# Second block: VectorE in program order, and what waits for ScalarE emitted later

## The chip, the cores and the metric

The kernel runs on one core of a Trainium2 chip. The metric is the device time of one launch in microseconds; a figure for a kernel is the median of its runs. TensorE (PE) multiplies matrices and transposes, VectorE (DVE) and ScalarE (ACT) work element by element, GpSimd (POOL) does some of that too, and SyncE (SP) issues the loads and stores. A matmul writes to one of eight PSUM banks, from which VectorE and ScalarE read.

## The reference, cut to what matters

Two transformer-like blocks run one after the other on x of shape (1, 512, 1024), in float32. The first has an RMS norm, a mixer (a chunked mLSTM beside stick-breaking attention) and an MLP with a squared ReLU. The change lies in the second, which is attention in three branches over 16 heads and 4 groups of keys and values:

```python
def second_block(x, ...):
    u = rms_norm_2(h, pre_norm_gain[layer])
    y = nsa_mixer(u, ...)
    return h + rms_norm_2(y, post_norm_gain[layer])

def nsa_mixer(h, w_in, w_out, k_pos, k_w1, k_w2, v_pos, v_w1, v_w2, table):
    q, kv, g, z = split_cols(h @ w_in, [NSA_WIDTH, 6 * NSA_KV_WIDTH, 3 * H, 3 * NSA_WIDTH])
    k_c, v_c, k_s, v_s, k_w, v_w = [a.reshape(B, S, G, dh) for a in jnp.split(kv, 6, axis=-1)]
    gates = jax.nn.sigmoid(g).reshape(B, S, 3, H, 1)
    zs = jax.nn.silu(z).reshape(B, S, 3, H, dh)
    kc = compress_kv(k_c, k_pos, k_w1, k_w2)      # blocks of 32 positions, silu(flat @ w1) @ w2
    vc = compress_kv(v_c, v_pos, v_w1, v_w2)
    o_cmp, p_cmp = nsa_compressed(q, kc, vc, table)
    sel = select_blocks(p_cmp, S)
    o_slc = nsa_selected(q, k_s, v_s, sel, table)
    o_win = nsa_window(q, k_w, v_w, table)
    o = jnp.stack([o_cmp, o_slc, o_win], axis=2)
    y = jnp.sum(gates * o * zs, axis=2).reshape(B, S, NSA_WIDTH)
    return y @ w_out
```

At 512 positions the selected branch takes all blocks and the window covers all earlier positions, so both are plain causal attention with a bias by distance, each with its own keys and values.

## The kernel before

**Matmuls in three parts.** To keep float32 accuracy each operand is split in a high half (a rounded copy) and a low half (what is left), and a product is three matmuls: high by high, high by low, low by high. Weights come in tiles of 128 by 1024: SyncE starts the load (tile wr), ScalarE makes the high half (wh, L171), VectorE the low half (wl, L173), from the 143rd tile on GpSimd in VectorE's place.

**Order.** A scheduler lays out the instructions of each engine by its own estimate of when they can run, which need not be the order in which the code emits them. The second block, nsa(), stands under `tc.manual_schedule` for TensorE and GpSimd: these two run in the order of the code there. VectorE, ScalarE and SyncE are laid out by the scheduler.

**The start of nsa().** The code first opens its pools, which lie in memory that the MLP's pools have left, and emits the memset of gz (L838) and two operations that fill gsel (tt, recorded at the helper's line 292). Much later come enter(0) and enter(1), each for half of the positions. enter adds two sums of squares (q), takes a mean (rsm, L286), has GpSimd raise it to the power -1/2 (rsr), scales the input in place (xbig, L284), has TensorE transpose it (L814) and splits the result into ah (ScalarE, L299) and al (VectorE, L289). The first three projections run half by half (half_step, L828). keys_evac, queries_evac and values move projections out of PSUM and split them (w2t at L852 is one such copy). attention() then clears the upper parts of two bias tiles (bt, L1290) and starts its loop.

**The loop of attention().** 8 pairs of heads, 2 branches, 2 heads and 4 blocks of 128 queries make 128 ticks. In a tick, u.scores multiplies queries by keys into one of two banks (L1213, L1214), VectorE adds the bias and takes the row minimum (nm, L1216), and ScalarE takes the exponential (P, L1219). Then come half of the tick's filler work, the flip of the block from two ticks earlier, the other half, and the mix of a half that was flipped at least MLAG ticks ago. A flip transposes P into one of two banks (L1233), ScalarE copies the high half into ptall (L1236), VectorE subtracts for the low half (ptall, L292). A mix multiplies with the values (L1249); after its second half ScalarE copies one part of the result (t1, L1255) and VectorE adds the other, the join. attended(p) then lets GpSimd multiply the pair's output with its gate.

**The filler** is the rest of the block, cut into steps of about 650 ns of TensorE. project(p, br) makes the gate z of a pair and a branch: a projection (three matmuls per weight tile, L332 to L334), a tanh on ScalarE (z, L991), and one VectorE operation (stt, recorded at L289) that multiplies it with the projection. compress makes 16 additions on VectorE (F_) for each of keys and values, four to a tile, while project(0, 1) and project(0, 2) run. cmp_scores, cmp_shift, cmp_exp, cmp_gate and cmp_flip are the compressed branch. Once a pair has all its row sums (dn), gate_rows takes the reciprocal (gs, L1118), multiplies with the gates and writes gz; gate_flip transposes gz (L1131) and gate_scale multiplies z by it. Such jobs wait in a list until a condition holds, counted in filler ticks; `started` is set after the second of the two compress stretches.

**The end.** The output projection's squares (ScalarE), row means m and products with the gain (yg, VectorE), GpSimd's power, and the sum with the residual.

Of the kernel before, what the change touches and what calls it, by code (L numbers as in the profile page):

```python
# [251 lines left out]
def tile_blocks(ctx, tc, x, xt, wts, prm, cst, table, post_g, w2k, w2v, out):  # L252
# [528 lines left out]
    def nsa(x2, ssq2):  # L781
# [4 lines left out]
        with ExitStack() as pts:  # L786
# [195 lines left out]
            def project(p, br):  # L982
                if (p, br) in zt:
                    return
                while live[0] == ZB:
                    yield None
                live[0] += 1
                z = pt.tile([128, T], F32, name="z", tag="z", bufs=ZB)

                def evac(ps):  # L990
                    s.activation(z, ps, AF.Tanh, scale=0.5)  # L991
                    stt(z, z, 1.0, ps, OP.add, OP.mult)
                yield from gen_t(pj, acts, evac)
                zt[p, br] = z
# [64 lines left out]
            def cmp_exp(gq):  # L1059
                P = pct["p", gq]  # L1060
                s.activation(P, P, AF.Exp, scale=-1.0)
                v.reduce_sum(den[:, :, 4 * gq:4 * gq + 4], P.rearrange("p (t r) c -> p t r c", t=4), AX.X)

            def cmp_gate(gq):
                P = pct["p", gq]
                r = small([128, 4, 4], "rgc")
                h4 = slice(4 * gq, 4 * gq + 4)
                v.reciprocal(r, den[:, :, h4])
                tt(r, r, gn[:, :, h4])
                tt(P, P, r.rearrange("p t r -> p (t r)")[:, :, None].to_broadcast([128, 16, 32]))  # L1070
# [129 lines left out]

            class Unit:
# [21 lines left out]
                def flip(self, tb):  # L1223
# [13 lines left out]
                    tt(PTl[:, 0:tb + 1, 128 * i:128 * i + 128], src, hi.bitcast(F32), OP.subtract)  # L1237

                def mix(self, half):
# [12 lines left out]
                    if half == 1:  # L1252
                        a = slice(0, 64) if self.h % 2 == 0 else slice(64, 128)
                        b = slice(64, 128) if self.h % 2 == 0 else slice(0, 64)
                        s.copy(self.t1[a, :], o[a, :])  # L1255
                        tt(self.t1[a, :], self.t1[a, :], o[b, :], OP.add)

            def attention(fill):
# [13 lines left out]
                def mixes(limit=MLAG):  # L1272
                    if len(pend_mix) > 0 and (tick[0] >= pend_mix[0][2] + limit):
                        u, half, _ = pend_mix.pop(0)
                        u.mix(half)
                        if u.h % 2 == 1 and u.br == 1 and half == 1:
                            attended(u.h // 2, u.ots)
# [22 lines left out]
                for p in range(8):  # L1300
# [8 lines left out]
                    for br in range(2):  # L1309
                        t1 = pt.tile([128, T], F32, name="t1", tag="ot", bufs=4)  # L1310
                        ots.append(t1)
                        for e in range(2):
                            u = Unit(2 * p + e, br, bt, t1, dn)
                            u.ots = ots
                            for tb in range(4):
# [3 lines left out]
                                u.scores(tb)  # L1319
                                fill.run(ns / 2)  # L1320
                                new = flips(LAG)
                                fill.run(ns / 2)
                                mixes()
# [4 lines left out]
                    fill.soon(lambda p=p, dn=dn: p - 1 in gated and started[0], lambda p=p, dn=dn: gate_rows(p, dn))  # L1328
                while pend_flip or pend_mix:
                    tick[0] += 1  # L1330
                    new = flips(0)
                    fill.run(ns)
                    mixes()
                    pend_mix += new

# [23 lines left out]
        with tc.tile_pool(name="pf", bufs=1) as pf:  # L1359
# [8 lines left out]
            for c in range(2):  # L1368
                ps = proj_n(pj, ys, 1 + 2 * c)
                for tb in range(4):  # L1370
# [4 lines left out]
                    step = v.tensor_scalar(m, ssq[:, c, tb:tb + 1], 1.0 / D, EPS if c == 0 else means[tb],  # L1375
                                           OP.mult, OP.add)
                    if c == 0:
                        means.append(m)
                        tt(yg[:, tb, cs], ps[tb], gb_[:, cs])
                    else:  # L1380
                        with tc.issue_after(step.ins):
                            tt(yg[:, tb, cs], ps[tb], gb_[:, cs])
# [9 lines left out]
    with tc.manual_schedule(engines={mybir.EngineType.PE, mybir.EngineType.Pool}):  # L1392
        nsa(xb, sums2)
# [55 lines left out]
```

## Time and profile before

| what | value |
|---|---|
| median of 3 runs | 1370.91 us (1369.25, 1370.91, 1371.4) |
| the profiled execution | 1371.08 us |
| its span in the trace | 1369.4 us |
| mean granted TensorE clock, share of full speed | 0.993 |
| TensorE busy | 1324.5 us, 97% |
| VectorE busy | 720.9 us, 53% |
| ScalarE busy | 655.6 us, 48% |
| GpSimd busy | 273.8 us, 20% |

The span runs from the first to the last instruction that the profiler recorded; the 1.7 us by which the execution is longer lie around it. The first block ends, and the second begins, at about 870 us. Busy shares are means over all stages. What the time depends on is read from the windows and the order of time, where an instruction's idle time before it stands in brackets with what released it.

### The profile page before, as it was taken

To read this page: it belongs to the slowest core of one execution; us is meant where nothing else is said; L and a number is where in the kernel's file an instruction comes from. 1 tells how busy PE (TensorE), PEld (TensorE's weight loads), DVE (VectorE), ACT (ScalarE), POOL (GpSimd) and SP (SyncE) were. 2 spreads that over 40 slices of the span, in tenths; PEclk is the share of its full clock that TensorE was granted. 3 is DMA by queue.
4 is the path that set the end of the run, shared out by engine and by line. 5 is a ranking of instruction groups with operands and counts; after the bars stand their busy time and mean duration, and the time that the engine had idled before them with its cause. 6 is when DMAs were issued, how large, how long until landed. Compare 5 with 4: busy or idle time off the path is not lost.

```text
span 1369.4 us, 17872 instructions
## 1 busy us (share of the span) xinstructions
PE 1324.5 (97%) x6670; PEld 1091.6 (80%) x6670; DVE 720.9 (53%) x1354; ACT 655.6 (48%) x1281; POOL 273.8 (20%) x243
## 2 busy tenths in 40 slices
PE   9999999999999999999999999999889999999998
PEld 7977887777786888888888888888767788888776
DVE  4589435656567535342233322544775766665623
ACT  6588624544434316351135512345556566665532
POOL 0023101110101000000000000145536344335342
PEclk9999999999999999999999999999999999999999
DMA  7411231223131424862333224313313112222132
GB/s 236 139 46 48 77 93 51 88 62 93 47 107 47 154 62 133 122 186 92 95 102 96 93 92 125 126 60 124 100 49 113 50 62 65 68 62 62 47 109 77
DMA packets 40694, 125.30 MB, mean 92 GB/s; under 512 B 4528, under 2 KB 9184, under 8 KB 40352
## 3 DMA queue, kind: packets, MB, share of 16 engines
q1 hardware_dynamic: 39696, 119.98, 28.0%
q0 software_dynamic: 912, 4.19, 2.3%
q8 instruction: 52, 0.85, 0.3%
q14 instruction: 34, 0.28, 0.1%
HBM read 115.77 MB, written 8.39 MB: 91 GB/s over the span
## 4 chain that ended last, share of the span: by engine, by line
PE 70%; issue 15%; DVE 8%; ACT 4%; POOL 2%; DMA 1%; POOLq 0%; DVEq 0%; SPq 0%; ACTq 0%
PE b L365 10%; PE b L367 10%; PE b L366 10%; PE b L332 10%; PE b L333 9%; PE b L334 9%; PE b L1249 2%; PE b L1233 2%; PE b L1213 1%; PE b L1214 1%; PE b L828 1%; DVE ptall L292 1%; ACT P L1219 1%; DVE b L1216 1%; POOL ssr L292 1%
## 5 line engine op out<-in xcount | busy, mean ns | idle before, releaser
L171 ACT CAST wh<-wr 128x1024 fp32r<-128x1024 f32 (+3 forms) x204 | 207.7, 1019 | 404.6 <-PE b L367 225.1
L332 PE MATMUL b<-ah,wh 128*128 128x512 f32 x808 | 332.1, 411 | 2.6 <-ACT w2t L852 2.2
L173 DVE TENSOR_TENSOR wl<-wr,wh 128x1024 fp32r<-128x1024 f32 (+2 forms) x142 | 169.4, 1194 | 297.1 <-ACT wh L171 296.6
L334 PE MATMUL b<-ah,wl 128*128 128x512 f32 x808 | 317.4, 393 | 0.0
L333 PE MATMUL b<-al,wh 128*128 128x512 f32 x808 | 317.2, 393 | 0.0
L173 POOL TENSOR_TENSOR wl<-wr,wh 128x1024 fp32r<-128x1024 f32 (+1 forms) x62 | 141.6, 2289 | 190.3 <-ACT wh L171 166.3
L334 PEld LDWEIGHTS b<-ah,wl 128*128 128x128 f32 x808 | 152.3, 189 | 32.6
L332 PEld LDWEIGHTS b<-ah,wh 128*128 128x128 f32 x808 | 152.8, 189 | 30.3 <-ACT w2t L852 2.5
L333 PEld LDWEIGHTS b<-al,wh 128*128 128x128 f32 x808 | 153.0, 189 | 25.5 <-issue 1.9
L365 PE MATMUL b<-wh,ah 128*128 128x512 f32 (+3 forms) x352 | 126.1, 360 | 1.9 <-ACT wh L171 1.9
L366 PE MATMUL b<-wl,ah 128*128 128x512 f32 (+3 forms) x352 | 125.8, 357 | 0.0
L367 PE MATMUL b<-wh,al 128*128 128x512 f32 (+3 forms) x352 | 125.8, 357 | 0.0
L1219 ACT ACTIVATE P<-b,nm 128x128 f32<-128x128 f32 (+3 forms) x128 | 67.6, 528 | 77.8 <-DVE nm L1216 73.7
L367 PE MATMUL b<-wh,hl 128*128 128x512 f32 x256 | 101.2, 396 | 0.0
L366 PE MATMUL b<-wl,hh 128*128 128x512 f32 x256 | 101.2, 395 | 0.0
L365 PE MATMUL b<-wh,hh 128*128 128x512 f32 x256 | 101.2, 395 | 0.0
L292 DVE TENSOR_TENSOR ptall<-b,ptall 128x128 fp32r<-128x128 f32 (+3 forms) x128 | 62.4, 489 | 65.1 <-ACT ptall L1236 64.3
L1216 DVE CUSTOM_DVE_ANT_0 b<-b,bt 128x128 f32<-128x128 f32 (+3 forms) x128 | 63.2, 495 | 28.0 <-PE b L1214 27.7
L365 PEld LDWEIGHTS b<-wh,ah 128*128 128x128 f32 x352 | 66.6, 190 | 9.8 <-ACT wh L171 2.1
L367 PEld LDWEIGHTS b<-wh,al 128*128 128x128 f32 x352 | 66.7, 189 | 8.5 <-DVE al L289 0.3
L366 PEld LDWEIGHTS b<-wl,ah 128*128 128x128 f32 x352 | 66.8, 190 | 8.2
L292 POOL TENSOR_TENSOR rsr<-rsm,mhalf 128x2 f32<-128x2 f32 (+1 forms) x3 | 2.4, 806 | 336.4 <-DVE rsm L286 336.4
(301 smaller groups left out, 2153.6 us busy)
## 6 DMA issues: line engine op xcount, KB each, us to landing
wr<-in_wts_dram SPq DMA_DIRECT2D x188, 512.0 KB, 3.6
bt_d<-tr POOLq DMA_DIRECT2D x4, 768.0 KB, 21.6
wr<-in_wts_dram SPq DMA_DIRECT2D x8, 280.0 KB, 2.6
xk<-in_xt_dram SPq DMA_DIRECT2D x8, 256.0 KB, 3.9
xn<-in_x_dram SPq DMA_DIRECT2D x4, 512.0 KB, 4.7
xbig<-in_x_dram SPq DMA_DIRECT2D x1, 2048.0 KB, 9.8
x_d<-xbig SPq DMA_DIRECT2D x8, 256.0 KB, 2.8
bt<-bt_d SPq DMA_DIRECT2D x8, 256.0 KB, 3.2
```

The lines of the kernel that those rows point to most:

```text
L171: nc.scalar.copy(hi, raw)
L173: eng.tensor_tensor(lo, raw, hi.bitcast(F32), OP.subtract)
L292: (eng or v).tensor_tensor(out_, a, b, op)
L332: pe.matmul(o, a, ah, start=(kt == 0), stop=False)
L333: pe.matmul(o, a, al, start=False, stop=False)
L334: pe.matmul(o, b, ah, start=False, stop=(kt == KT - 1))
L365: pe.matmul(o, ah[:, tsl], a, start=(kk == 0 and k == 0), stop=False)
L366: pe.matmul(o, ah[:, tsl], b, start=False, stop=False)
L367: W.last = pe.matmul(o, al[:, tsl], a, start=False, stop=end)
L1216: v.tensor_tensor_reduce(S[:, 0:n], S[:, 0:n], self.bt[:, h % 2, 512 - n:512], 1.0, -NEG, OP.add, OP.min, nm)
L1219: latest[0] = s.activation(P[:, 0:n], S[:, 0:n], AF.Exp, bias=nm, scale=-1.0, accum_out=self.dn[:, tb, br, h % 2:h % 2 + 1])
L1233: pe.transpose(pst[:, 128 * sb:128 * sb + 128], P[:, 128 * sb:128 * sb + 128], ident)
```

## The change

It has five parts. Nothing is removed, and no operation, shape or buffer differs.

- nsa() runs VectorE, too, in the order of the code.
- In project, the VectorE operation that makes z is emitted when the projection's generator has ended and not inside it, and in the compressed branch the row sum moves from cmp_exp to cmp_gate.
- A list `later` takes the flip's low half and the mix's join. catch_up() emits what is in it: in each tick right after the scores and again after the second half of the filler, and likewise in the loop behind the last tick. attended() now runs with the join.
- gate_rows comes at least two filler ticks after its pair's last tick.
- In the last rows yg is emitted ahead of m, in both column halves, and no longer held behind m.

```diff
@@ -987,10 +987,13 @@
                 live[0] += 1
                 z = pt.tile([128, T], F32, name="z", tag="z", bufs=ZB)
 
+                got = []
+
                 def evac(ps):
                     s.activation(z, ps, AF.Tanh, scale=0.5)
-                    stt(z, z, 1.0, ps, OP.add, OP.mult)
+                    got.append(ps)
                 yield from gen_t(pj, acts, evac)
+                stt(z, z, 1.0, got[0], OP.add, OP.mult)
                 zt[p, br] = z
 
             zt = {}
@@ -1059,11 +1062,11 @@
             def cmp_exp(gq):
                 P = pct["p", gq]
                 s.activation(P, P, AF.Exp, scale=-1.0)
-                v.reduce_sum(den[:, :, 4 * gq:4 * gq + 4], P.rearrange("p (t r) c -> p t r c", t=4), AX.X)
 
             def cmp_gate(gq):
                 P = pct["p", gq]
                 r = small([128, 4, 4], "rgc")
+                v.reduce_sum(den[:, :, 4 * gq:4 * gq + 4], P.rearrange("p (t r) c -> p t r c", t=4), AX.X)
                 h4 = slice(4 * gq, 4 * gq + 4)
                 v.reciprocal(r, den[:, :, h4])
                 tt(r, r, gn[:, :, h4])
@@ -1198,6 +1201,12 @@
                     if br == 0 and p % 2:
                         fill.soon(lambda: p in pct, lambda: finish(p))
 
+            later = []
+
+            def catch_up():
+                while later:
+                    later.pop(0)()
+
             class Unit:
                 def __init__(self, h, br, bt, t1, dn):
                     self.h, self.br, self.bt, self.t1, self.dn = h, br, bt, t1, dn
@@ -1234,7 +1243,7 @@
                     src = pst[:, 0:n].rearrange("p (a b) -> p a b", b=128)
                     hi = PTh[:, 0:tb + 1, 128 * i:128 * i + 128]
                     s.copy(hi, src)
-                    tt(PTl[:, 0:tb + 1, 128 * i:128 * i + 128], src, hi.bitcast(F32), OP.subtract)
+                    later.append(lambda: tt(PTl[:, 0:tb + 1, 128 * i:128 * i + 128], src, hi.bitcast(F32), OP.subtract))
 
                 def mix(self, half):
                     if half == 0:
@@ -1253,7 +1262,12 @@
                         a = slice(0, 64) if self.h % 2 == 0 else slice(64, 128)
                         b = slice(64, 128) if self.h % 2 == 0 else slice(0, 64)
                         s.copy(self.t1[a, :], o[a, :])
-                        tt(self.t1[a, :], self.t1[a, :], o[b, :], OP.add)
+
+                        def join():
+                            tt(self.t1[a, :], self.t1[a, :], o[b, :], OP.add)
+                            if self.h % 2 == 1 and self.br == 1:
+                                attended(self.h // 2, self.ots)
+                        later.append(join)
 
             def attention(fill):
                 pend_flip, pend_mix = [], []
@@ -1273,8 +1287,6 @@
                     if len(pend_mix) > 0 and (tick[0] >= pend_mix[0][2] + limit):
                         u, half, _ = pend_mix.pop(0)
                         u.mix(half)
-                        if u.h % 2 == 1 and u.br == 1 and half == 1:
-                            attended(u.h // 2, u.ots)
 
                 def flips(limit):
                     if len(pend_flip) > limit:
@@ -1317,21 +1329,26 @@
                                 tick[0] += 1
                                 ns = FILL if p < 3 else fill.left / (steps + TAIL)
                                 u.scores(tb)
+                                catch_up()
                                 fill.run(ns / 2)
                                 new = flips(LAG)
                                 fill.run(ns / 2)
+                                catch_up()
                                 mixes()
                                 pend_mix += new
                                 pend_flip.append((u, tb))
                             if br == 0 and e == 1 and p < 7:
                                 load_bias(p + 1)
-                    fill.soon(lambda p=p, dn=dn: p - 1 in gated and started[0], lambda p=p, dn=dn: gate_rows(p, dn))
+                    fill.soon(lambda p=p, dn=dn, t0=fill.ticks: p - 1 in gated and started[0] and fill.ticks >= t0 + 2, lambda p=p, dn=dn: gate_rows(p, dn))
                 while pend_flip or pend_mix:
                     tick[0] += 1
+                    catch_up()
                     new = flips(0)
                     fill.run(ns)
+                    catch_up()
                     mixes()
                     pend_mix += new
+                catch_up()
 
             first = [(pj(), W.next(1), keys_evac(0)), (pj(), W.next(1), queries_evac(0)),
                      (mx(), W.next(1), queries_evac(1))]
@@ -1372,14 +1389,11 @@
                     jk = glob.tile([128, T], F32, name="jk3", tag="wr", bufs=3)
                     s.activation(jk, ps[tb], AF.Square, accum_out=ssq[:, c, tb:tb + 1])
                     m = pf.tile([128, 1], F32, name="m", tag=f"m{c}{tb}")
-                    step = v.tensor_scalar(m, ssq[:, c, tb:tb + 1], 1.0 / D, EPS if c == 0 else means[tb],
-                                           OP.mult, OP.add)
+                    tt(yg[:, tb, cs], ps[tb], gb_[:, cs])
+                    v.tensor_scalar(m, ssq[:, c, tb:tb + 1], 1.0 / D, EPS if c == 0 else means[tb], OP.mult, OP.add)
                     if c == 0:
                         means.append(m)
-                        tt(yg[:, tb, cs], ps[tb], gb_[:, cs])
                     else:
-                        with tc.issue_after(step.ins):
-                            tt(yg[:, tb, cs], ps[tb], gb_[:, cs])
                         r = small([128, 1], "frr")
                         tt(r, m, mhalf[:, 0:1], OP.pow, eng=g)
                         for d in range(2):
@@ -1389,7 +1403,7 @@
 
     xb = first_mixer()
     sums2 = mlp(xb)
-    with tc.manual_schedule(engines={mybir.EngineType.PE, mybir.EngineType.Pool}):
+    with tc.manual_schedule(engines={mybir.EngineType.PE, mybir.EngineType.Pool, mybir.EngineType.DVE}):
         nsa(xb, sums2)
 
 
```

## Rows read from the trace of the kernel before

**Rows 1.** The page: busy time by engine; the chain that ended last, by engine.

```profile
PE 1324.5 (97%) x6670; PEld 1091.6 (80%) x6670; DVE 720.9 (53%) x1354; ACT 655.6 (48%) x1281; POOL 273.8 (20%) x243
...
PE 70%; issue 15%; DVE 8%; ACT 4%; POOL 2%; DMA 1%; POOLq 0%; DVEq 0%; SPq 0%; ACTq 0%
```

**Rows 2.** Windows: us, busy PE, PEld, DVE, ACT, POOL (count), PEclk, DMA share, GB/s.

```profile
960.00:970.00 10.00, 7.50 (x34) 5.89 (x34) 9.71 (x18) 3.41 (x9) 2.68 (x4) 0.84 0.12 45
...
1020.00:1030.00 10.00, 5.08 (x25) 4.48 (x26) 7.78 (x16) 5.86 (x14) 5.84 (x5) 0.74 0.00 0
1030.00:1040.00 10.00, 9.18 (x57) 7.91 (x57) 4.95 (x11) 3.83 (x8) 6.91 (x5) 0.92 0.46 122
...
1050.00:1060.00 10.00, 7.76 (x46) 6.44 (x45) 6.47 (x19) 7.60 (x19) 2.39 (x1) 1.00 0.24 61
```

**Rows 3.** Waits, 870 to end: who <- for whom: us in all, times, longest.

```profile
ACT P L1219 <- DVE nm L1216: 73.7, 74, 2.8
DVE ptall L292 <- ACT ptall L1236: 64.3, 72, 2.4
...
DVE z L289 <- ACT z L991: 14.7, 12, 2.1
...
ACT ah L299 <- DVE al L289: 4.9, 5, 2.4
...
PE b L828 <- DVE al L289: 1.9, 2, 1.1
```

**Rows 4.** VectorE in order of time, 864 to 886: start, us, what [idle before].

```profile
864.98 0.16 DVE L292 TENSOR_TENSOR q<-ssq 128x2 f32<-128x2 f32 x1 [0.85 <-ACT jk L777]
...
866.17 1.42 DVE L284 TENSOR_SCALAR xbig<-xbig,rsr 128x1024 f32<-128x1024 f32 x2 [0.83 <-POOL rsr L292]
...
871.51 2.56 DVE L173 TENSOR_TENSOR wl<-wr,wh 128x1024 fp32r<-128x1024 f32 x2 [1.79 <-ACT wh L171]
874.57 0.75 DVE L289 SCALAR_TENSOR_TENSOR xbig<-b,rs,xbig 128x512 f32<-128x512 f32 x1 [0.50 <-PE b L367]
875.30 0.18 DVE L838 MEMSET gz<- 128x152 f32 x1
875.41 1.62 DVE L292 TENSOR_TENSOR gsel<-ident 128x128 fp32r<-128x128 f32 x2
...
877.55 0.48 DVE L1290 MEMSET bt<- 128x512 f32 x1
...
879.18 2.57 DVE L284 TENSOR_SCALAR xbig<-xbig,rsr 128x1024 f32<-128x1024 f32 x1
```

**Rows 5.** TensorE in order of time, the first transposes of enter(0).

```profile
874.37 1.91 PE L814 MATMUL b<-ident,xbig 128*128 128x128 f32 x16
```

**Rows 6.** GpSimd in order of time, a weight split in the same stretch.

```profile
878.80 2.40 POOL L173 TENSOR_TENSOR wl<-wr,wh 128x1024 fp32r<-128x1024 f32 x1
```

**Rows 7.** TensorE in order of time, the two stretches with the F_ additions.

```profile
966.66 0.66 PE L1213 MATMUL b<-kh,q 128*128 128x384 f32 x1 [2.50 <-ACT P L1219]
...
975.97 0.33 PE L1213 MATMUL b<-kh,q 128*128 128x128 f32 x1 [1.63 <-ACT P L1219]
...
1027.10 1.09 PE L1131 MATMUL b<-ident,gz 128*128 128x128 f32 x4 [4.01 <-DVE ptall L292]
```

**Rows 8.** VectorE in order of time, the same stretches.

```profile
988.14 0.25 DVE L1118 RECIPROCAL gs<-dn 128x16 f32<-128x16 f32 x1 [1.28 <-ACT P L1219]
...
1009.34 2.18 DVE L292 TENSOR_TENSOR F__8253<-w2t,pr 64x248 f32<-64x248 f32 x2
...
1021.76 3.16 DVE L292 TENSOR_TENSOR F__8349<-w2t,pr 64x248 f32<-64x248 f32 x4
```

**Rows 9.** VectorE, then TensorE, in order of time, the tail of attention.

```profile
1311.59 0.69 DVE L289 SCALAR_TENSOR_TENSOR z<-z,b 128x512 f32<-128x512 f32 x1 [1.62 <-ACT z L991]
...
1313.64 0.66 PE L1131 MATMUL b<-ident,gz 128*128 128x128 f32 x4 [1.84 <-DVE ptall L292]
```

**Rows 10.** VectorE in order of time, the last rows.

```profile
1363.88 0.68 DVE L292 TENSOR_TENSOR yg<-b,gb__11524 128x512 f32<-128x512 f32 x1
```

## The prediction, made before the changed kernel was run

> **What bounds the kernel now.** I read the page first: TensorE is busy for 97% of the span and holds 70% of the chain that ended last [rows 1]. So the time moves only where TensorE waits, or where its clock falls. Then the windows of 10 us over the second block, to find where that is; four of them stand in [rows 2], and in them the reader is to compare PE's busy time with the 10 us and to look at the granted clock. Outside such windows TensorE is full, and there an idle VectorE or ScalarE costs nothing. The totals of the waits [rows 3] are large between VectorE and ScalarE (64.3 us of VectorE on the high halves of the flips, 73.7 us of ScalarE on the row minima), but nearly all of that is slack: a flip is used some two ticks after its scores, a mix two ticks after its flip. The change aims at those 64.3 us, and they are not worth 64.3 us. What counts is which instruction TensorE stands at when it does wait, so I went to the order of time on VectorE and TensorE around each window [rows 4 to 10].
>
> **The change part by part.**
>
> *1. The start of the block, which the diff does not mention.* With VectorE in program order, the first VectorE instructions of nsa() are, by the code, the memset of gz (L838) and the two operations on gsel; enter(0) comes after them. Today VectorE runs them the other way round: q at 864.98 and the scaling of xbig from 866.17 to 867.59, beside the last matmuls of the MLP; gz at 875.30 and gsel from 875.41 to 877.03 [rows 4]. Why so late? The memset reads nothing, and VectorE stood idle for 1.79 us ahead of the weight split at 871.51 [rows 4]. What is left is its memory: gz and gsel lie in a pool that is opened after the MLP's pool is closed, and gz ran straight after the operation at 874.57 that had waited for TensorE's last MLP matmul. I take it that gz can't start before that. Then enter(0) is pushed behind it: gsel ends at 877.03; from q's start to the end of the scaling it takes 867.59 - 864.98 = 2.61 us; so xbig is ready at 879.64, and TensorE's first transposes, today at 874.37 [rows 5], start 5.27 us later. TensorE has nothing else to do, since its own order is by program too. Bounds: 0 if gz can run before 864.98; and 5.27 + 1.86 if the scaling meets a weight split of GpSimd, as it does at 879.18 (2.57 us, with the split at 878.80 beside it, against 1.42 / 2 = 0.71) [rows 4, 6]. I take +5.3, as at 866.17, since GpSimd's next split comes after both of the block's powers in its own program order.
>
> From there to the transposes of enter(1) the same work remains. TensorE loses its 1.9 us of waits for low halves (al) [rows 3], because bt's memsets, q and rsm no longer stand between them; against that, enter(1)'s scaling now comes after all eight al and meets the split. Bounds -1.9 and +1.9 (the collision again); I take +0.2. Front: +5.5.
>
> *2. TensorE's clock after that gap.* At 1020 to 1030 a wait of 4.01 us goes with a granted clock of 0.74 and the next 10 us with 0.92; at 960 to 970 one of 2.50 us with 0.84; at 1050 to 1060 2.2 us idle with 1.00 [rows 2, 7]. Lost: 10 x (1 - 0.74) = 2.6 us, 0.8, 1.6 and nothing. After the front gap TensorE soon waits for enter(1) again, and slow matmuls ahead of a wait cost little. Bounds 0 and 3.4; I take +1.0.
>
> *3. bt's memsets.* Today the first runs at 877.55 (0.48 us) in the shade of the start [rows 4]; by program both come after values(), ahead of the first reduction. 2 x 0.48 = 0.96 us on the way to the first exponential, for whose bank the third score waits; bounds 0 and 0.96, I take +0.9.
>
> *4. The stretches with the F_ additions* (about 957 to 975 and 1009 to 1027). Here TensorE waits 2.50 and 1.63 us for exponentials and 4.01 us for a bank [rows 7]; these are the largest waits of the block. But VectorE has no gap there: two additions take 2.18 us at 1009.34, four take 3.16 us at 1021.76 [rows 8], 32 of them in all by the code, two for every three matmuls of a projection. Read against the code, they already stand about where the program has them. An order can't remove work, so I take 0 for it. What the change moves: low halves of flips go behind the next additions (later), reductions come ahead by one low half. And pair 0's gate_rows, which runs from 988.14 now [rows 8], is emitted only once `started` is set, in the second stretch; its four operations (0.25 us for the first) then stand ahead of the gate's transposes at 1027.10: 4 x 0.25 = +1.0. Bounds -6.6 (half of the waits of [rows 7], 8.1 us, and of the clock lost with them, 5.0 us) and +2 (the four twice).
>
> *5. The rest of attention.* Deferring flips' subtractions, joins and the z products by half a tick to a tick costs nothing while mixes come two ticks later. That cover hangs on the ring of two PSUM banks for the transposes, which a low half frees. The reductions of the compressed branch, which now run as early as they can, spread out. I take -1.0. Nothing in the trace shows the new order, so the bounds are a third of the 14.7 us that VectorE idles for z today [rows 3], either way: -4.9 and +4.9.
>
> *6. The tail.* Now a z product that waits for ScalarE (1.62 us idle before 1311.59) and a join stand ahead of the two last low halves, and the last gate's transposes wait 1.84 us for the bank [rows 9]. In the new order the low halves don't stand behind that, and gate_rows and the transposes come a tick later: -2.0; bounds -3.5 (with the 1.62) and 0. The gate's chain gets later by two runs; the output projection's first six heads hide that, and without them it would cost what it is late.
>
> *7. The last rows.* yg (0.68 us) now precedes m; today it lies behind m, beside GpSimd's power [rows 10]. If yg may read its bank beside ScalarE's square, nothing changes: bounds 0 and +0.68. The nearest rows are two pairs of halves that share a bank: ScalarE waits 4.9 us for al ahead of ah [rows 3], so I take +0.5. The Trainium skill, "PSUM — Partial Sum Buffer", section "PSUM bank collisions raise a hardware error", says that any two engines on one bank, two readers too, have to be kept apart. By that rule this term is the upper end, +0.68, and without it 0; the waits of ScalarE for al agree with the rule.
>
> Sum: 5.5 + 1.0 + 0.9 + 1.0 - 1.0 - 2.0 + 0.5 = +5.9. The profiled execution took 1371.08 us (span 1369.4), 0.17 above the median of 1370.91. 1371.08 + 5.9 = 1377.0.
>
> **The rivals.** *Forecast*: a new wait of TensorE at the start takes more than the order gives back: 1377.0 (1373 to 1381), chance 0.55.
> *A gain*: the waits of the F_ stretches are a matter of order after all, and reductions in their place let TensorE run on. Price: three quarters of the waits of [rows 7] and of the clock lost with them, 0.75 x (8.1 + 5.0) = 9.8, with the tail's 2.0, against 5.5 + 0.9 + 0.5: 1371.08 - 4.9 = 1366.2. It decides from the point where those waits shrink by more than the 6.9 us of the front, the memsets and the end. For it: two of the three waits are for exponentials, so for reductions. Against: VectorE is full there. Chance 0.22.
> *It hardly does anything*: gz's memory is free before 864.98, so the front and its clock cost nothing: 0.9 + 1.0 - 1.0 - 2.0 + 0.5 = -0.6, 1370.5. Against it: gz's place today. Chance 0.13.
> *Order as a wait*: VectorE now stands at every product that needs ScalarE (24 z; 14.7 us idle at 12 of them today [rows 3]) with reductions queued behind; ScalarE's exponentials wait for those, TensorE for the exponentials. If a third of another 14.7 us reaches TensorE, 4.9 on top of the forecast: 1381.9. Chance 0.10.
>
> **How the numbers follow.** The time is that of the likeliest, 1377.0. A measurement of this kernel tells about 0.2% (2.7 us) from no change: faster means under 1368.2, slower over 1373.6. Faster: the gain, 0.22. Same: the third rival and a small part of the forecast, 0.13 + 0.05 = 0.18. Slower: 0.50 + 0.10 = 0.60. Range: from within the gain, 1365.0, to the fourth rival with 2 us of its bounds, 1384.0.
>
> **What would show it.** Front: gz and gsel ahead of q, and the first L814 transposes some 5 us after the MLP's last matmul; if they follow it within 1 us, part 1 is wrong. Clock: a window under 0.9 right after. F_ stretches: VectorE still full, TensorE still waiting some 8 us at these instructions; if that falls under 4 us, part 4 is wrong. Tail: the gate's transposes without a wait. End: m after yg. VectorE's 64.3 us on ptall fall to a fraction in any case, and that alone shows nothing of the time.

## The result

The changed kernel takes 1404.78 us (four runs, 1404.52 to 1405.1) against 1370.41 for the kernel before: 1.0252 of its time, 95% interval 1.0235 to 1.0268. That is 34.4 us slower, where 6 were forecast and 13 were the end of the range. The profiled execution has a span of 1402.9 us, 33.5 longer than before.

First the page, as in [rows 1]: busy time by engine, and the chain that ended last.

```profile
PE 1335.8 (95%) x6670; PEld 1098.8 (78%) x6670; DVE 727.9 (52%) x1354; ACT 658.2 (47%) x1281; POOL 273.9 (20%) x243
...
PE 66%; issue 16%; DVE 10%; ACT 5%; POOL 2%; DMA 1%; SPq 0%; POOLq 0%; DVEq 0%; ACTq 0%
```

TensorE runs the same 6670 matmuls and is busy for 1335.8 - 1324.5 = 11.3 us more: that is the clock, granted at 0.983 of full speed on average in place of 0.993. The other 33.5 - 11.3 = 22.2 us of the span are waits. To find where, I took the start of each of the 128 score products of attention() from TensorE's order of time in both traces and looked at the difference:

| score (from 0) | before, us | after, us | difference | what came in between |
|---|---|---|---|---|
| 0 | 940.7 | 946.5 | +5.8 | the start of the block |
| 2 | 944.9 | 951.8 | +6.9 | bt's memsets |
| 28 | 1022.7 | 1028.5 | +5.8 | the two stretches with the F_ additions |
| 29 | 1032.1 | 1042.0 | +9.8 | the gate's transposes of pair 0 |
| 34 | 1047.1 | 1063.7 | +16.5 | the same of pair 1 |
| 81 | 1179.5 | 1201.0 | +21.5 | small steps of 0.3 to 1.1 |
| 82 | 1183.5 | 1212.7 | +29.2 | the gate's transposes of pair 4 |
| 115 | 1274.4 | 1302.7 | +28.4 | |
| 117 | 1279.1 | 1312.1 | +33.0 | a gate product behind cmp_shift |
| 127 | 1306.4 | 1339.2 | +32.9 | |
| last matmul | 1362.9 | 1395.8 | +32.9 | the tail and the output projection |
| end of the span | 1369.4 | 1402.9 | +33.5 | the last rows |

Four jumps make 23 of the 33 us: at the gate's transposes of pairs 0, 1 and 4 and behind cmp_shift. Only pair 0's had a term of its own in the forecast, of 1 us. The windows of 10 us show three of them and the start; the columns are those of [rows 2], with PEclk third from the end.

```profile
870.00:880.00 10.00, 5.44 (x24) 4.12 (x22) 6.54 (x10) 4.84 (x7) 3.06 (x2) 0.85 0.69 223
880.00:890.00 10.00, 9.39 (x65) 9.22 (x64) 6.87 (x12) 3.07 (x8) 3.07 (x2) 0.81 0.20 68
...
1030.00:1040.00 10.00, 2.61 (x10) 2.35 (x11) 7.49 (x13) 4.31 (x10) 5.87 (x3) 0.53 0.35 103
...
1060.00:1070.00 10.00, 9.82 (x45) 8.45 (x46) 4.73 (x15) 3.31 (x9) 0.00 (x0) 0.76 0.09 39
...
1200.00:1210.00 10.00, 4.95 (x28) 4.19 (x26) 6.70 (x12) 6.04 (x12) 2.48 (x1) 0.73 0.18 54
1210.00:1220.00 10.00, 10.00 (x45) 8.51 (x46) 4.59 (x12) 3.44 (x8) 0.00 (x0) 0.75 0.00 0
```

From 1030 to 1040 TensorE works 2.61 of 10 us and the granted clock is 0.53, close to the lower of its two levels (1.2 of 2.4 GHz). After such a wait the clock stays low for a while: from 1060 and from 1210 TensorE is nearly full, and the mean is 0.76 and 0.75. So a wait costs more than its length: 5.05 us of waiting at 1207.51, the only wait there, made 7.7 us between scores 81 and 82.

What TensorE stood at, from its order of time (the columns are those of [rows 5], with the idle time before and its releaser in brackets):

```profile
878.00 0.48 PE L814 MATMUL b<-ident,xbig 128*128 128x128 f32 x1 [4.38 <-DVE xbig L284]
...
1037.39 0.87 PE L1134 MATMUL b<-ident,gz 128*128 128x128 f32 x3 [8.50 <-DVE gz L292]
...
1060.18 1.12 PE L1134 MATMUL b<-ident,gz 128*128 128x128 f32 x4 [5.37 <-DVE ptall L292]
...
1207.51 0.90 PE L1134 MATMUL b<-ident,gz 128*128 128x128 f32 x3 [5.05 <-DVE ptall L292]
...
1305.95 0.47 PE L1144 MATMUL b<-gT,gsel 128*128 128x512 f32 x1 [2.53 <-DVE ptall L292]
```

Three of the five are the gate's transposes (gate_flip, now L1134). Behind the first of them lies this, in VectorE's order of time and then GpSimd's, the place where [rows 7] had a wait of 4.01 us:

```profile
1032.18 0.69 DVE L1225 CUSTOM_DVE_ANT_0 b<-b,bt 128x512 f32<-128x512 f32 x1
1032.79 0.14 DVE L1225 DVE_READ_ACCUMULATOR2_ANT nm<- 128x1 f32 x1
1032.79 0.25 DVE L1121 RECIPROCAL gs<-dn 128x16 f32<-128x16 f32 x1
1033.07 1.67 DVE L292 TENSOR_TENSOR gs<-gs,gn 128x16 f32<-128x16 f32 x1
1034.77 2.26 DVE L1125 CAST gz<-gs 128x16 fp32r<-128x16 f32 x1
1037.07 0.17 DVE L292 TENSOR_TENSOR gz<-gs,gz 128x16 fp32r<-128x16 f32 x1
1037.16 0.28 DVE L292 TENSOR_TENSOR ptall<-b,ptall 128x128 fp32r<-128x128 f32 x1
1037.36 0.29 DVE L1225 CUSTOM_DVE_ANT_0 b<-b,bt 128x128 f32<-128x128 f32 x1
...
1032.36 4.65 POOL L173 TENSOR_TENSOR wl<-wr,wh 128x1024 fp32r<-128x1024 f32 x2
```

gate_rows' four operations on 16 numbers a partition take 4.35 us, about half of the wait of 8.50, and the next low half and reduction stand behind them. The third ends at 1037.03 and GpSimd's two splits at 1037.01; the second, at 1034.74, ends where the first split does, some 2.3 us after 1032.36. The reciprocal, in the middle of that split, takes its usual 0.25. At pair 4 it is the same with one split, and ahead of it VectorE stood for ScalarE's copies of the keys:

```profile
1203.07 1.39 DVE L292 TENSOR_TENSOR kl<-w2t,kh 64x512 fp32r<-64x512 f32 x2 [0.52 <-ACT kh L859]
1204.48 0.25 DVE L1121 RECIPROCAL gs<-dn 128x16 f32<-128x16 f32 x1
1204.77 1.93 DVE L292 TENSOR_TENSOR gs<-gs,gn 128x16 f32<-128x16 f32 x1
1206.73 0.17 DVE L1125 CAST gz<-gs 128x16 fp32r<-128x16 f32 x1
1206.94 0.18 DVE L292 TENSOR_TENSOR gz<-gs,gz 128x16 fp32r<-128x16 f32 x1
1207.03 0.42 DVE L292 TENSOR_TENSOR ptall<-b,ptall 128x256 fp32r<-128x256 f32 x1
...
1204.19 2.48 POOL L173 TENSOR_TENSOR wl<-wr,wh 128x1024 fp32r<-128x1024 f32 x1 [10.70 <-ACT wh L171]
```

At the fourth jump it is the subtraction of cmp_shift, ahead of the low half for whose bank TensorE waits. It runs beside a GpSimd addition from 1303.38 to 1304.66 and takes 1.74 us, where the one at 1153.71, with nothing beside it, takes 0.69:

```profile
1303.47 1.74 DVE L292 TENSOR_TENSOR Pc<-Pc,mns 128x512 f32<-128x512 f32 x1
```

In the kernel before, the scheduler had put reductions and low halves in between such operations. That gave two theories: the fixed order does it (P), or the later emission, which puts low halves behind the filler, does it (D).

### The profile page after: what moved, and what is told of

It is laid out like the page before. It is cut to its first block, busy times and chain, and to the rows that moved or that the text cites. A ratio compares the mean times of both kernels' runs of the same rounds, so it can differ in the third digit from the quotient of the medians.

```text
span 1402.9 us, 17851 instructions
## 1 busy us (share of the span) xinstructions
PE 1335.8 (95%) x6670; PEld 1098.8 (78%) x6670; DVE 727.9 (52%) x1354; ACT 658.2 (47%) x1281; POOL 273.9 (20%) x243
## 4 chain that ended last, share of the span: by engine, by line
PE 66%; issue 16%; DVE 10%; ACT 5%; POOL 2%; DMA 1%; SPq 0%; POOLq 0%; DVEq 0%; ACTq 0%
PE b L332 9%; PE b L365 9%; PE b L367 9%; PE b L333 9%; PE b L366 9%; PE b L334 9%; PE b L1258 2%; PE b L1242 2%; PE b L1222 1%; DVE ptall L292 1%; PE b L1223 1%; DMA xk<-in_xt_dram 1%; ACT wh L171 1%; ACT P L1228 1%; DVE kl L292 1%
## 5 line engine op out<-in xcount | busy, mean ns | idle before, releaser
L1228 ACT ACTIVATE P<-b,nm 128x128 f32<-128x128 f32 (+3 forms) x128 | 67.7, 529 | 95.2 <-DVE nm L1225 93.9
L292 DVE TENSOR_TENSOR ptall<-b,ptall 128x128 fp32r<-128x128 f32 (+3 forms) x128 | 62.5, 489 | 59.0 <-ACT ptall L1245 58.1
L1242 PE MATMUL b<-ident,P 128*128 128x128 f32 x320 | 57.5, 279 | 10.2 <-DVE ptall L292 10.1
```

The source lines that it names most:

```text
L292: (eng or v).tensor_tensor(out_, a, b, op)
L1228: latest[0] = s.activation(P[:, 0:n], S[:, 0:n], AF.Exp, bias=nm, scale=-1.0, accum_out=self.dn[:, tb, br, h % 2:h % 2 + 1])
L1242: pe.transpose(pst[:, 128 * sb:128 * sb + 128], P[:, 128 * sb:128 * sb + 128], ident)
```

## The experiments

**Which of the two parts.** e1 is the kernel before with only the last line of the diff, e2 the changed kernel without it.

```diff
-    with tc.manual_schedule(engines={mybir.EngineType.PE, mybir.EngineType.Pool}):
+    with tc.manual_schedule(engines={mybir.EngineType.PE, mybir.EngineType.Pool, mybir.EngineType.DVE}):
         nsa(xb, sums2)
```

> The kernel before with one edit: VectorE runs nsa() in the order of the code; nothing is emitted later and gate_rows, z, the row sums and yg stand where they stood. Theory P (program order itself costs the 34 us: the filler's VectorE work, which waits for ScalarE and is stretched beside GpSimd's weight splits, stands ahead of low halves and reductions): 1400 us or more, as slow as the changed kernel or slower, with waits of TensorE of 4 us and more at the gate's transposes, since the low halves now also make VectorE wait. Theory D (the later emission costs it: a low half that stood right behind its flip is put behind half a tick of filler): 1376 to 1385, the start's 6 us and little else.

> The changed kernel with one edit: VectorE is laid out by the scheduler again, so that all that is emitted later is so, but the order of the code does not bind. Theory P: the start is as before and so are the long waits at the gate's transposes; within 3 us of the kernel before, 1368 to 1374. Theory D: the scheduler follows the order of emission where nothing speaks against it, so that low halves run later and TensorE waits for the transposes' banks; 1380 to 1400.

e1: 1400.25 us, ratio 1.0216 [1.0195, 1.0236]. e2: 1369.67 us, ratio 0.9992 [0.9983, 1.0002]. The fixed order alone costs 30 us; what is emitted later costs nothing that can be measured where the scheduler lays out VectorE, and 4.5 us more where it does not. P stands. e1 shows the same waits, 9.35 and 3.91 us for gz at the transposes of pairs 0 and 1; at pair 4 it is 2.69 us, at a flip.

**The low halves at once**, in program order:

```diff
-                    later.append(lambda: tt(PTl[...], src, hi.bitcast(F32), OP.subtract))
+                    tt(PTl[...], src, hi.bitcast(F32), OP.subtract)
```

> The changed kernel with the flip's low half emitted at once, right behind ScalarE's high half, as before the change; joins stay later. Theory P: VectorE now also stands at each of 128 high halves, with reductions behind; not faster than the changed kernel, 1403 to 1425. Theory D: low halves no longer stand behind gate_rows and the copies of keys and queries, so the three long waits at the gate's transposes (8.5, 5.4 and 5.1 us) shrink to those of before; 1383 to 1393.

1401.08 us, 3.7 less than the changed kernel: nearer to P's end, but outside both. Putting the low halves later cost 3.7 us in program order, since they then stand behind the second half of the filler. The waits at the gate's transposes stay (8.86, 4.67 and 4.80 us), now for gz.

**The start.** The memset of gz and the two operations on gsel move behind the first three projections.

> The changed kernel with the memset of gz and the two operations on gsel emitted after the first three projections, and so behind both enter(). Both theories, and step 1 of the prediction: the first transposes of enter(0) follow the last matmul of the MLP within 1 us in place of 4.4, and the whole is 4.5 to 8 us shorter than the changed kernel, 1397 to 1400: the bubble of 3.6 us by the traces and the clock that it costs. If it is under 2 us shorter, the gap at the start is hidden by something else.

1401.02 us, 3.8 less; 4.5 to 8 were expected. The gap ahead of the first transposes is gone, but another one opens at enter(1):

```profile
873.15 1.91 PE L814 MATMUL b<-ident,xbig 128*128 128x128 f32 x16
...
884.36 0.38 PE L814 MATMUL b<-ident,xbig 128*128 128x128 f32 x1 [2.83 <-DVE xbig L284]
```

enter(1)'s scaling starts at 881.39, beside a split of GpSimd from 881.33, and its two operations take 3.49 us where two took 1.42 at the start of [rows 4]. That is 8.2 us after the first of these transposes; the scheduler had it 4.8 us after them, at 879.18, beside a split too, and ahead of the last low halves.

**gate_rows: its distance, its place, its price.** e5 makes one number larger, e6 emits the four operations behind the next reduction and low half, e7 leaves them out.

```diff
-                fill.soon(lambda: fill.ticks >= t0 + 2, lambda: gate_flip(p))
+                fill.soon(lambda: fill.ticks >= t0 + 6, lambda: gate_flip(p))
```

> The changed kernel with one number changed: the gate's transposes (gate_flip) come 6 filler runs, three ticks, behind gate_rows in place of 2. Theory R (distance: in program order the four operations of gate_rows run late and slowly, and the transposes that need them are due one tick later, so TensorE stands there): the three waits of 8.5, 5.4 and 5.1 us at the gate's transposes shrink to 1 us or less each, and with the clock that they cost 12 to 20 us go, 1385 to 1393. Theory B (backlog: VectorE is behind there by all of the filler's work, and what TensorE meets next waits in place of the gate's transposes): the waits move to the next transposes of P, 1399 to 1405.

> The changed kernel with the four operations of gate_rows put in a list of their own that is emitted behind the next reduction and the low half, up to a tick later; the gate's transposes stay where they are. Theory R: gz comes later still, and TensorE waits for it as long or longer, 1402 to 1412. Theory B: low halves and reductions no longer stand behind the four, banks come free, 1388 to 1396.

> The changed kernel without the four VectorE operations of gate_rows, 32 in all; gz stays zero, so that this part of the computation is left out (the gates of two branches). It prices those operations where they stand. Theory R: the waits at the gate's transposes lose what gate_rows takes there (4.4, 3.1 and 2.6 us by the trace of the changed kernel) and the clock that goes with it; 1386 to 1394. Theory B: 1396 to 1402, since the copies of keys and queries and the F_ additions remain.

e5: 1390.15 us, 14.6 less, and e6: 1411.04 us, 6.3 more, both in R's ranges. e7: 1385.22 us, 19.6 less, just under R's. So most of the loss hangs on gate_rows, and on how close the transposes follow: three ticks of distance give back three quarters of what leaving it out gives. B is not empty, though. Even without gate_rows TensorE waits 3.44, 2.19 and 2.58 us for a bank at the gate's transposes of pairs 0, 1 and 4 (e7), and in e5 smaller waits come up at the flips behind:

```profile
1032.91 0.44 PE L1242 MATMUL b<-ident,P 128*128 128x128 f32 x2 [3.44 <-DVE ptall L292]
...
1058.26 1.11 PE L1242 MATMUL b<-ident,P 128*128 128x128 f32 x4 [4.20 <-DVE ptall L292]
```

**Repairs in program order.** e8 puts the start, the memsets, pair 0's gate_rows and the distance right; e9 also cuts the filler's blocks into pieces of one to three operations, one piece at each half tick; e13 counts the distance from where gate_rows is really emitted. (Where the expectations of e9 and e13 say pair 5, it is the fifth pair, p = 4.)

> The changed kernel with gz, gsel and the two bias memsets emitted behind both enter(), gate_rows of pair 0 as soon as its row sums are there (not held for the end of the second compress stretch), and the gate's transposes 6 filler runs behind it. Theory R: the start's 4 us, the memsets' 1 us and the three long waits go: 1370 to 1380. Theory B: 1390 or more.

> The kernel of e8_fixed, and besides it the filler's blocks of VectorE work (the four low halves of keys, the two of queries, the two operations of cmp_shift, the four of cmp_gate, the four of gate_rows) go into a list from which one item is emitted at each half tick, behind the low halves of flips. Theory B (what is left over the kernel before, 17 us in e8_fixed, is blocks that stand in one piece ahead of reductions and low halves): 1371 to 1379. Rival (any fixed order makes VectorE stand for ScalarE, whatever the blocks): 1383 to 1390.

> The kernel of e9_blocks, where the distance of the gate's transposes is counted from the point at which gate_rows is really emitted (4 filler runs, for the last pair 2) and not from its call, since in e9 the list delays it and the transposes of pair 5 stand right behind it (3.77 us of wait for gz, 6 us with the clock). If distance is what is left there: 1375 to 1379. If the wait only moves to a bank: 1382 to 1386.

1387.7, 1384.16 and 1384.14 us: none fulfils what the theory behind it promised, and 14 to 17 us stay over the 1370.41 of the kernel before. e8 lies between its two theories; e9 lies in the range of its rival, and e13 in the one for a wait that only moves to a bank. e13 shows one such place, pair 4 again, where it loses some 5 us, clock included, between scores 83 and 85 (VectorE, then GpSimd, then TensorE in order of time):

```profile
1198.56 1.92 DVE L1153 CAST gz<-gs 128x16 fp32r<-128x16 f32 x1
1200.51 0.18 DVE L292 TENSOR_TENSOR gz<-gs,gz 128x16 fp32r<-128x16 f32 x1
1200.61 0.28 DVE L292 TENSOR_TENSOR ptall<-b,ptall 128x128 fp32r<-128x128 f32 x1
...
1198.11 2.34 POOL L173 TENSOR_TENSOR wl<-wr,wh 128x1024 fp32r<-128x1024 f32 x1 [5.19 <-ACT wh L171]
...
1200.95 1.12 PE L1165 MATMUL b<-ident,gz 128*128 128x128 f32 x4 [2.56 <-DVE ptall L292]
```

gate_rows now comes in two pieces with a reduction in between, and still the cast to gz runs from 1198.56 until a split has ended, and in a fixed order the low half for whose bank TensorE waits is behind it.

**GpSimd's splits.** e10 is the changed kernel, e11 the kernel before, e15 the kernel of e13, each without the 62 splits:

```diff
-        eng = nc.gpsimd if self.loaded >= POOL_FROM else nc.vector
-        eng.tensor_tensor(lo, raw, hi.bitcast(F32), OP.subtract)
+        if self.loaded >= POOL_FROM:
+            lo = hi
 ...
```

> The changed kernel without GpSimd's 62 weight splits (from the 143rd tile on the high half is used for the low one too, so that this part of the computation is left out). Beside it the same cut in the kernel before, e11. Theory L (GpSimd's splits hold VectorE's operations on SBUF, so that gate_rows takes up to 4.4 us in place of 0.8, and that makes a good part of the long waits): the gap to the kernel before, 34 us, falls to 15 to 25 us between these two. Rival (the operations would be late anyway): the gap stays at 30 to 36 us.

> The kernel before with the same cut as e10, its counterpart: 1362 to 1371, since TensorE has few waits here that hang on a stretched operation; the F_ stretches gain 2 to 6 us if the splits and not the additions make them long.

> The kernel of e13_spaced without GpSimd's weight splits (the cut of e10 and e11, which leaves out the same part of the computation), to be set against e11 at 1362.2. If what is left in program order after the repairs, 13 us, is GpSimd holding operations that other work stands behind: 1362 to 1367. If it is the waits for ScalarE in a fixed order: 1371 to 1376.

These three leave out a part of the computation, and serve only to price the splits.

| kernel | with the splits | without | gain |
|---|---|---|---|
| before (e11) | 1370.41 | 1362.23 | 8.2 |
| changed (e10) | 1404.78 | 1378.46 | 26.3 |
| repaired (e13, e15) | 1384.14 | 1365.68 | 18.5 |

Without the splits the change costs 16.2 us in place of 34.4, and the repaired order 3.5 in place of 13.7. In e10 the instructions on gs and gz have one duration each (from the instructions of one tile; the three numbers are the shortest, the median and the longest in ns):

```profile
L1123 DVE RECIPROCAL gs<-dn x8: 240/248/254, 1022.8 to 1320.2; 128x16 f32<-128x16 f32 x8
L294 DVE TENSOR_TENSOR gs<-gs,gn x8: 174/175/176, 1023.1 to 1320.5; 128x16 f32<-128x16 f32 x8
L1127 DVE CAST gz<-gs x8: 174/175/176, 1023.3 to 1320.7; 128x16 fp32r<-128x16 f32 x8
```

In the changed kernel the same three are

```profile
L1121 DVE RECIPROCAL gs<-dn x8: 241/248/253, 1032.8 to 1345.5; 128x16 f32<-128x16 f32 x8
L292 DVE TENSOR_TENSOR gs<-gs,gn x8: 176/306/1931, 1033.1 to 1345.8; 128x16 f32<-128x16 f32 x8
L1125 DVE CAST gz<-gs x8: 174/176/2261, 1034.8 to 1346.0; 128x16 fp32r<-128x16 f32 x8
```

The waits at the gate's transposes of pairs 0, 1 and 4 fall from 8.50, 5.37 and 5.05 us to

```profile
1023.86 1.09 PE L1136 MATMUL b<-ident,gz 128*128 128x128 f32 x4 [4.92 <-DVE gz L294]
...
1043.78 0.66 PE L1136 MATMUL b<-ident,gz 128*128 128x128 f32 x4 [2.40 <-DVE ptall L294]
...
1185.28 1.11 PE L1136 MATMUL b<-ident,gz 128*128 128x128 f32 x4 [3.29 <-DVE ptall L294]
```

So about half of the loss, 18 of 34 us, is there only together with the splits, and 8.3 us of TensorE's waits at these three places, before the clock, go with the held operations. What stays is the order by itself: at pair 4 of e10 VectorE still stands 1.84 and 0.52 us for ScalarE's copies of the keys, with gate_rows and the low half behind. The cut also takes half of GpSimd's work away (133.5 of 273.9 us are left), and how much of the gain comes from a shorter queue there was not taken apart.

**Three attempts at a faster kernel**, all with VectorE left to the scheduler: e12 is e2 with the gate's transposes later, e14 the kernel before with half of the F_ additions on GpSimd, e16 with every second split on VectorE.

> The kernel of e2_defer_only (everything emitted later, VectorE laid out by the scheduler) with the gate's transposes 6 filler runs behind gate_rows in place of 2. If the wait of 3.5 us at the first of these transposes and its clock can be had this way: 1364 to 1368. If VectorE's additions make the next transposes wait as long: 1368.5 to 1371.

> The kernel before with half of the 32 F_ additions on GpSimd in place of VectorE; VectorE is the scheduler's, as before. If VectorE's additions in the two stretches bound them (step 4 of the prediction), 16 of 0.8 us go from it and TensorE's waits there, some 12 us with the clock, fall by half: 1362 to 1368. If GpSimd, which holds VectorE while it adds, gives that back: 1369 to 1376.

> The kernel before with every second of the 62 weight splits of GpSimd on VectorE. If the holding by GpSimd is worth more than VectorE's own work (31 splits of 1.2 us against 31 of 2.3 us in which it may be held): 1364 to 1369. If VectorE's load counts more in the full stretches: 1372 to 1382.

1370.55 us (1.0002 [0.9992, 1.0012]), 1370.76 us (0.9996 [0.9986, 1.0005]) and 1375.7 us (1.0037 [1.0027, 1.0046]). In e14 the wait of 4.01 us of [rows 7] is still 3.83. e16 is 0.4% slower, and none of the versions that compute the whole is faster than the kernel before by more than the noise.

## Why the prediction was wrong, point by point

The sign was right, and so was the order that step 1 read from the code. The size was wrong by 28 us, and the time lay 20.8 us outside the range.

*1, 2. The start and its clock.* Forecast +5.5 and +1.0; the first score came 5.8 us later, clock included. That the sum is so close is in part luck: the gap was 1.6 us shorter than forecast, and what the clock (0.85 and 0.81 in the first two windows above) and enter(1) cost was 1.0 us more, 2.2 for 1.2. The first transposes waited 4.38 us and came at 878.00, 3.6 us later than before and not 5.27, since gz started 0.9 us earlier than step 1 had it, and the transposes began behind the first of the two scalings:

```profile
874.40 0.18 DVE L838 MEMSET gz<- 128x152 f32 x1
874.50 1.60 DVE L292 TENSOR_TENSOR gsel<-ident 128x128 fp32r<-128x128 f32 x2
876.02 0.15 DVE L292 TENSOR_TENSOR q<-ssq 128x2 f32<-128x2 f32 x1
876.20 0.17 DVE L286 TENSOR_SCALAR rsm<-q 128x2 f32<-128x2 f32 x1
877.20 1.42 DVE L284 TENSOR_SCALAR xbig<-xbig,rsr 128x1024 f32<-128x1024 f32 x2 [0.82 <-POOL rsr L292]
```

e3 prices it at 3.8 us, since part of it comes back at enter(1). *3. bt's memsets*: +0.9 forecast, +1.0 measured. *7. The last rows*: +0.5 forecast, 33.5 - 32.9 = +0.6 measured. yg starts when ScalarE's square on the same bank has ended:

```profile
1396.66 0.69 DVE L292 TENSOR_TENSOR yg<-b,gb__11524 128x512 f32<-128x512 f32 x1 [1.22 <-ACT jk L1390]
1397.27 0.21 DVE L1393 TENSOR_SCALAR m<-ssq,m 128x1 f32<-128x1 f32 x1
```

e2 has the same +0.6, and e1, where m stays first, has none. This is the upper end that the rule of the Trainium skill cited in step 7 gave. *6. The tail*: -2.0 forecast, 0 measured (scores 127 to the last matmul): the gate's transposes wait 1.30 us in place of 1.84, and a mix waits for a join in their place.

*4. gate_rows of pair 0* is the first step that failed, as a mis-sized term. It was priced "4 x 0.25 = +1.0", by the reciprocal of [rows 8]. The four took 4.35 us, and from score 2 to score 29 the loss grew by 2.9 us, past the bound of +2. The row that says so stood in the trace of before, one line behind the one that was read: the next operation on gs took 1.52 us there, beside a split. The group of that tile in the trace of before has it too:

```profile
L292 DVE TENSOR_TENSOR gs<-gs,gn x8: 164/174/1516, 988.4 to 1309.1; 128x16 f32<-128x16 f32 x8
...
L292 DVE TENSOR_TENSOR gz<-gs,gz x8: 166/175/1142, 991.5 to 1309.8; 128x16 fp32r<-128x16 f32 x8
```

The collision with GpSimd was weighed for xbig, in step 1, and for nothing else. The two F_ stretches themselves did what step 4 said: an order took no work out of them. Score 28 is 5.8 us late, as score 0 was, so they gave back 1 us, no more.

*5. "The rest of attention"* is the second, and the larger: -1.0 with bounds of 4.9 either way, against 32.9 - 9.8 = 23.1 us by the table (the jumps of pairs 1 and 4 and of cmp_shift, and the small steps). Its sentence that the deferral "costs nothing while mixes come two ticks later" is true where the scheduler orders (e2); in program order the later low halves cost 3.7 us (e4). But the bounds were taken from VectorE's idle time for z, and the question was another: which of the filler's operations will stand in one piece ahead of a low half, how long it can take, and how soon TensorE is due. gate_rows comes for every pair, and the price of pair 0 was never carried to the others. The rival "order as a wait" came nearest, in that a fixed order makes others stand behind a VectorE that waits for ScalarE. But its place was the 24 products of z, and VectorE's waits for z rose only from 14.7 [rows 3] to 17.7 us; the wait of this kind that counted was for the keys' copies, 1.84 and 0.52 us at pair 4. ScalarE's waits for the row minima rose, too, from 73.7 to 93.9 us:

```profile
ACT P L1228 <- DVE nm L1225: 93.9, 78, 5.0
DVE ptall L292 <- ACT ptall L1245: 58.1, 59, 2.4
...
DVE z L289 <- ACT z L993: 17.7, 14, 2.0
```

Of the signs to look for, those of the front, the clock and the end held. In the F_ stretches TensorE waited on, at other instructions: 2.42 us at a flip at 972.44, 8.50 us at 1037.39. Two signs failed: the tail's transposes still waited, and the 64.3 us of [rows 3], which were to "fall to a fraction in any case", fell to 58.1 only.

What the runs leave: about 20 us at gate_rows (e7), 4 at the start (e3), 4 for the low halves put later (e4), 0.6 at the end. These overlap and are not a sum. Across them, 18 us need GpSimd's splits (e10 against e11). In the repaired order 10 of 13.7 us need them (e15). The last 3.5, which rest on two and three runs, were not traced further.

## What to carry to other kernels

Before an engine that a scheduler orders is put in program order, list every operation that the code emits ahead of one for which TensorE waits, and price each by the longest duration in its own group, not by the median and not by its neighbour: in order, the longest is what everything behind it pays. Give what TensorE needs a distance of some ticks from the operations that make it, or let the scheduler keep the order; a large total of waits between two engines that are not the bound is no reason to change it.

## What was not expected of the hardware

While GpSimd works on two tiles in SBUF, a VectorE operation that reads two tiles there, or a cast from one to another, ends only after GpSimd's. For 16 numbers a partition, 174 ns became 1931, and a cast's 174 became 2261; in both cases the end is some 0.03 us behind that of a split. What it loses is what is left of GpSimd's operation, whatever its own size. Not held were the reciprocal (241 to 253 ns in all eight), the minimum of cmp_shift (0.68 us at 1302.75, in a split from 1301.03 to 1303.43) and operations with an input from PSUM (z, 0.69 us at 1301.55, in the same split). The Trainium skill, "SBUF — State Buffer", section "Who interferes with whom", says that the two engines share a pair of ports under an exclusive lock, that two inputs in SBUF or a copy or cast in a two-port mode contend for it, and that a reduction on this chip never does. The rows agree in what is held and what is not; the ports themselves no run shows. By e10 and e11 the splits were worth 26 us in one order of the same operations and 8 in another, the effect of GpSimd's shorter queue included.
